# Hybrid streaming-encoder layer: y's halves split sooner, B's additions a step later, bias tiles made apart from their load, eight fillers moved to A's first step, the last tile in pieces

## The chip, the cores and the metric

The kernel runs on one core of a Trainium2 chip. The metric is the device time of one execution in microseconds (us). The engines are PE (TensorE, matmuls and transposes), DVE (VectorE), ACT (ScalarE), POOL (GpSimd) and SP (SyncE, which issues all DMAs of this kernel). Each engine works through its own queue in order.

## The reference

One post-norm layer with 1024 positions, width 1024, float32. Two token mixers run on the same input, A over bands of 9 chunks of 64 with a bias by distance, B with stick-breaking weights, 8 heads of 64 each; then gates, projections, two layer norms and a SwiGLU of width 2816.

```
h = x @ w_in[l]
qa, ka, va, qb, kb, vb, ga, gb = jnp.split(h, split_pts, axis=-1)
y_a = chunk_band_attention(heads_a(qa), heads_a(ka), heads_a(va), rel_bias[l]) @ w_proj_a[l]
y_b = stick_breaking_attention(heads_b(qb), heads_b(kb), heads_b(vb)) @ w_proj_b[l]
mix = (sigmoid(ga + b_gate[l, :D]) * y_a + sigmoid(gb + b_gate[l, D:]) * y_b) @ w_out[l]
x = layer_norm(alpha * x + mix, ln1_g[l], ln1_b[l])
g, u = jnp.split(x @ w_ffn_in[l], 2, axis=-1)
x = layer_norm(alpha * x + (silu(g) * u) @ w_ffn_out[l], ln2_g[l], ln2_b[l])
```

In `chunk_band_attention` the scores get `bias = rel_bias[:, idx]` with the clipped distance as index, then a softmax. In `stick_breaking_attention` the weight of position s at t is sigmoid(z_ts) times the product of (1 - sigmoid(z_tj)) over s < j < t; each is then multiplied with v.

## The kernel before

**Precision.** Every float32 operand is split into a high part (ACT casts it to fp32r) and a low part (DVE or POOL subtracts the high part from the raw one), and a product is three matmuls: high by high, high by low, low by high. `split`, line 108, does this with ACT and DVE; `split_y`, line 798, with ACT and POOL.

**Stages.** In order of time: the input projections (to about 343 us of the span), the attention of 16 heads (to about 660), the projection of B and the output projection with the first layer norm, the SwiGLU's upward part, and its downward part with the second layer norm, eight tiles of 128 rows each, at the end.

**The attention.** The loop at line 856 goes over 16 heads (8 of A, then 8 of B) with 12 steps each: 8 steps of group 0 (queries 0 to 511) and 4 of group 1 (512 to 1023). A step stands for one block of 128 keys. Its `turn` transposes the weights of up to 4 query blocks on PE into a `tr` bank and splits the result into a `pt` tile (4 of them); its `mult` multiplies this tile with v into the single `pv` bank. A `mult` waits in `pend` until LAG = 2 later steps have been written down. At the second step of a group of A, one `mult` is popped ahead of the turn. The last `mult` of a group has ACT copy the `pv` bank (line 704), one half of the copy goes through a DMA to other partitions (line 705), and `add` has POOL add it to the rest (line 708). `add` is put off in the list `later`, whose items count down at each step, three steps before. For pairs 5 and 6 `add` puts `split_y` into the same list, 6 and 8 steps on.

The weights themselves are made ahead by `wunits`, one unit for one block of 128 queries: `soft_block` for A (scores on PE, bias and minimum on DVE, exponential on ACT, division on POOL) and `stick_block` for B (scores on PE, two sigmoids on ACT, a scan on DVE, and a product on POOL, line 649). `LEAD` says how many units are written down by each step; the fourth unit of a B head is written down at step 8 of the head before, four steps ahead of its first transpose. A's fifth to eighth are similarly early; the first block of a head is written down at step 2 of the head before.

**The bias tile of a head of A** (`rel_bias_tile`, line 577) is loaded by one DMA into a tile `braw`; ACT writes it reversed and negated into `bias`; POOL sets two corners. This is part of `load_qk`, called at step 8 for the head after the next. Both tiles come from the four `kp` slots.

**Fillers.** PE gets other matmuls in between: 480 of them, one at a time from the generator `fill_all` (line 721). The first 288 make the gates 10 to 15 (`gate`, line 473; 48 each, with the next gate's weights split half-way through each), the other 192 the projection of A's result y (line 761, `yAps`, 24 for each of 8 columns, halves LO and HI of the positions). `FILL` gives their number for each head, spread evenly over its 12 steps. The last gate lets go of the split x tiles, and `freed` puts the split halves of y0 to y3 into their slots: the lower halves while its k = 2 to 5 are done, and the upper halves by `pieces`, from which two are taken in the gate and two in the first column's projection (line 764).

**Order.** The program is written in this order, but a planner (the scheduler of the framework) sets each engine's order from it: at each point it takes the earliest written instruction that its own cost model holds ready, so that fillers and loads can move far ahead of their place. `tc.keep_in_program_order` puts an instruction behind the one written before it on its engine; `split_y` and the gates' weights use it. The order on an engine is then fixed.

**The end.** `down_plain` (line 1151) makes a tile of 128 rows in two halves of 512 columns, 12 matmuls each; DVE adds each half to the residual. `layer_norm` (line 930) has DVE take statistics of the two halves, POOL raise the variance to the power -1/2, and, for the last tile (`quick`), DVE finish each half, which a DMA then stores.

Of the kernel before, what the change touches and what calls it, by code (L numbers as in the profile page):

```python
# [18 lines left out]
P = 128  # L19
# [18 lines left out]

FILL = (18, 18, 18, 18, 18, 18, 18, 36, 42, 42, 40, 40, 40, 38, 38, 38)

# [7 lines left out]
def hybrid_trunk_kernel(ctx: ExitStack, tc, x, xt, w_in, b_gate, rel_bias, w_proj,  # L48
# [424 lines left out]
    def gate(i, w, half_way, freed=None):  # L473
# [13 lines left out]
        if freed is None:  # L487
            for hf in range(2):
                if hf:
                    acc.append(bank("mm", f"gps{i}_1"))  # L490
                    half_way()
                for k in range(KT):
                    yield from part(hf, k)
                take(hf)
        else:
            half_way()
            for k in range(6):
                for hf in range(2):
                    yield from part(hf, k)
                freed(k)  # L500
            for hf in range(2):
                for k in (6, 7):
                    yield from part(hf, k)
                take(hf)
                freed(6 + hf)
        dma(g_dr[i], gt)
# [33 lines left out]
    def load_qk(hd):  # L540
# [11 lines left out]
        if hd["br"] == 0:  # L552
            hd["bias"] = rel_bias_tile(hd["n"])

# [21 lines left out]

    def rel_bias_tile(head):
        braw = slot("kp", f"braw{head}")
        src = rel_dr[head:head + 1, 0:640]
        dma(braw[:, 0:640],  # L580
            bass.AP(tensor=src.tensor, offset=src.offset, ap=[[1, P], [1, 640]]))
        bias = slot("kp", f"bias{head}")
        nc.scalar.activation(bias[:, 0:640], braw[:, 0:640][:, ::-1], AF.Copy, scale=-1.0)  # L583
        nc.gpsimd.memset(bias[0:DH, 576:640], BIG)  # L584
        nc.gpsimd.memset(bias[DH:P, 0:DH], BIG)
        return bias

# [65 lines left out]
    def value_steps(hd, g, wt):  # L653
# [9 lines left out]
        for i, kb in enumerate(kbs):  # L663
# [14 lines left out]
            def mult(i=i, kb=kb, lo_q=lo_q, n=n, pts=pts):  # L678
# [8 lines left out]
                if last:  # L687
# [10 lines left out]
                    else:  # L698
# [8 lines left out]
                        def add():  # L707
                            nc.gpsimd.tensor_tensor(yt[r, gs], yt[r, gs], yv[r, gs], ALU.add)
                            if h == 1 and g == 1:
# [3 lines left out]
                                else:  # L713
                                    dma(y_dr[hd["i"]], yt)
                        later.append([3, add])

# [4 lines left out]
    def fill_all():  # L721
# [23 lines left out]
        for cc in range(4):  # L745
            if cc < 3:
                end = begin_proj(0, cc + 1)
            for j in range(2):
# [5 lines left out]
                for hf, cs in enumerate((LO, HI)):  # L754
# [3 lines left out]
                    for k in range(4):  # L758
                        ks = slice(j * HW + k * P, j * HW + (k + 1) * P)
                        for n, (lw, rx) in enumerate(((w[0], yh), (w[0], yl), (w[1], yh))):  # L760
                            mm(acc, lw[:, ks], rx[k][:, cs], start=(k == n == 0),  # L761
                               stop=(k == 3 and n == 2))
                            yield 1.0
                        if k % 2 and pieces:
                            pieces.pop(0)()
# [86 lines left out]
    goal = 0.0  # L852
    load_qk(heads[0])
    load_qk(heads[1])
    load_v(heads[0])
    for si, (hd, g, st, box) in enumerate(vsteps):
        hidx, pos = si // nhead, si % nhead
        if hidx < 14 and pos == 8:
            load_qk(heads[hidx + 2])
        if pos == 4:  # L860
            if hidx < 15:
# [5 lines left out]
        while wi < min(hidx * 8 + LEAD[hd["br"]][pos], len(wunits)):  # L867
            wunits[wi]()
            wi += 1
        if st == 0:  # L870
            steps_of[(hidx, g)] = value_steps(hd, g, box)
# [10 lines left out]
        pend.append(mult)  # L882
        if len(pend) > LAG:
            pend.pop(0)()
# [44 lines left out]

    def layer_norm(t, g, b, name, quick, done=lambda cs: None):  # L930
        st = sml.tile([P, 12], F32, name=f"bn_{name}", tag="bn")
        mv = sml.tile([P, 3], F32, name=f"mv_{name}", tag="mv")
        for hf in range(2):
            nc.vector.bn_stats(st[:, 6 * hf:6 * hf + 6], t[:, hf * HW:(hf + 1) * HW])
        nc.vector.bn_aggr(mv[:, 0:2], st)
        nc.vector.tensor_scalar(mv[:, 2:3], mv[:, 1:2], EPS, None, ALU.add)  # L936
# [213 lines left out]

    def down_plain(hs, tt, evac):
        ts_ = slice(tt * P, (tt + 1) * P)
        for hf, cs in enumerate((LO, HI)):
            acc = bank("mm" if hf == 0 else "tr", f"fps{hs[0][0].name}_{tt}_{hf}")
            mm3(acc, [(hh[:, ts_], hl[:, ts_], oh[:, cs], ol[:, cs]) for hh, hl, oh, ol in hs])
            evac(acc_t[tt][:, cs], acc)
# [101 lines left out]
    for tt in range(8):  # L1258
        down_plain(last, tt, add_to)
        layer_norm(acc_t[tt], *norm2, f"2_{tt}", tt == 7,  # L1260
                   lambda cs: dma(out[tt * P:(tt + 1) * P, cs], acc_t[tt][:, cs]))

# [33 lines left out]
```

## Time and profile before

| | |
|---|---|
| median of three runs | 1446.99 us (1446.37 to 1449.32) |
| profiled execution, its own time | 1448.6 us |
| its span | 1446.8 us |
| mean granted clock of TensorE over it | 0.998 |
| busy shares: PE, DVE, ACT, POOL | 99%, 71%, 47%, 19% |

Times in the profile's rows are us from the span's start. A row of a timeline gives the start, the duration, engine and line, the operation with its output and input, its shape, and in brackets the idle time of the engine before it with what ended it. A row of the waits says which engine and line waited for which, how long in all, how often, and the longest. A row of windows gives busy time of each engine in a stretch of the span, and the granted clock. Matmuls overlap in the rows: their ends are modelled, and the distance of starts is what a matmul costs. A group's row (line, engine, operation, shapes) gives the busy time in all and the mean in ns, then the idle time before it.

### The profile page before, as it was taken

The numbers are of one execution on the slowest core, as the hardware profiler recorded it, in microseconds if no ns is written. First come the engines' busy times: TensorE is split into PE (matmuls) and PEld (weight loads), VectorE is DVE, ScalarE is ACT, GpSimd is POOL, SyncE is SP. The second block draws the span as 40 slices with busy tenths as digits, with TensorE's granted clock in tenths as the row PEclk, the third lists the DMA queues.
The fourth block names the chain that finished last, engine by engine and source line by source line (L and its number), as shares of the span: only waits on it lengthen the run. The fifth ranks groups of instructions, "written<-read, shape, count | busy, mean of one in ns | idle before, by whom it ended". The sixth has DMA issues, their size and how long they took to land.

```text
span 1446.8 us, 19239 instructions
## 1 busy us (share of the span) xinstructions
PE 1428.1 (99%) x6748; PEld 1182.8 (82%) x6748; DVE 1029.5 (71%) x1649; ACT 679.5 (47%) x1193; POOL 269.2 (19%) x329
## 2 busy tenths in 40 slices
PE   9999999999999999999999999999999999999997
PEld 7888888888788887888888888888888888888886
DVE  8875566545777777886759966776777755988767
ACT  6444444545878787773413633444444433221201
POOL 0000000001555777860004000000000000100016
PEclk9999999999999999999999999999999999999999
DMA  7555657758767477858602133444444457787502
GB/s 248 156 179 175 174 178 230 264 188 243 213 200 201 137 244 227 255 174 288 206 30 88 56 115 113 142 158 160 160 149 154 148 200 252 291 310 239 206 15 102
DMA packets 87777, 262.95 MB, mean 182 GB/s; under 512 B 10992, under 2 KB 10992, under 8 KB 87680
## 3 DMA queue, kind: packets, MB, share of 16 engines
q1 hardware_dynamic: 87680, 261.72, 54.7%
q8 instruction: 53, 0.87, 0.2%
q14 instruction: 44, 0.36, 0.1%
HBM read 169.89 MB, written 88.11 MB: 178 GB/s over the span
## 4 chain that ended last, share of the span: by engine, by line
PE 93%; DVE 3%; ACT 1%; issue 1%; DMA 1%; POOL 0%; SPq 0%; POOLq 0%; DVEq 0%; ACTq 0%
PE sxf L179 16%; PE sxp L179 11%; PE szf L179 8%; PE dx L1228 6%; PE szp L179 5%; PE syf L179 4%; PE gps L480 4%; PE syp L179 3%; PE dz L1228 3%; PE yAps L761 3%; PE tp_b L672 2%; PE ops L116 2%; PE ops L119 2%; PE ops L117 2%; PE tp_a L672 2%; PE fpswh_h L119 2%
## 5 line engine op out<-in xcount | busy, mean ns | idle before, releaser
L1184 POOL TENSOR_TENSOR wdyt<-wdyt 128x512 f32<-128x512 f32 x8 | 11.2, 1394 | 512.3 <-ACT h L1057 422.6
L649 POOL TENSOR_TENSOR w_b<-w_b,kp_b 128x511 f32<-128x511 f32 (+3 forms) x96 | 96.1, 1013 | 36.9 <-DVE kp_b L644 18.0
L644 DVE TENSOR_TENSOR_SCAN kp_b<-kp_b,ident_ps 128x512 f32<-128x512 f32 (+2 forms) x64 | 56.5, 884 | 27.0 <-ACT kp_b L641 26.6
L641 ACT ACTIVATE kp_b<-sc_b 128x512 f32<-128x512 f32 (+3 forms) x96 | 48.0, 500 | 34.7 <-PE sc_b L567 32.3
L937 POOL TENSOR_TENSOR mv<-mv,neghalf 128x1 f32<-128x1 f32 x16 | 23.9, 1495 | 207.8 <-DVE mv L936 207.8
L194 DVE TENSOR_TENSOR c<-sxp,c 128x512 f32<-128x512 f32 x16 | 11.1, 691 | 72.0 <-PE sxp L179 43.1
L584 POOL MEMSET bias<- 64x64 f32 x8 | 1.2, 144 | 326.9 <-ACT bias L583 326.9
L179 PE MATMUL szf<-x1S63h,wcf 128*128 128x512 f32 x168 | 55.1, 389 | 0.0
L110 DVE TENSOR_TENSOR pt_b<-tp_b,pt_b 128x512 fp32r<-128x512 f32 (+1 forms) x96 | 50.0, 544 | 6.3 <-ACT pt_b L109 5.6
L1159 DVE TENSOR_TENSOR x<-dx,x 128x512 f32<-128x512 f32 x64 | 43.4, 686 | 14.9 <-PE dx L1228 14.9
L614 POOL TENSOR_SCALAR w_a<-w_a,st_a 128x640 f32<-128x640 f32 (+2 forms) x64 | 42.4, 667 | 58.2 <-PE sc_a L567 25.1
L109 ACT CAST pt_b<-tp_b 128x512 fp32r<-128x512 f32 (+1 forms) x96 | 47.2, 500 | 10.3 <-PE tp_b L672 9.9
L110 DVE TENSOR_TENSOR pt_a<-tp_a,pt_a 128x512 fp32r<-128x512 f32 (+1 forms) x96 | 45.0, 486 | 9.6 <-ACT pt_a L109 8.8
L110 DVE TENSOR_TENSOR sl<-h,sl 128x512 fp32r<-128x512 f32 x56 | 38.4, 685 | 18.8 <-ACT sl L109 18.8
L109 ACT CAST sl<-h 128x512 fp32r<-128x512 f32 x56 | 34.7, 619 | 33.2 <-PE syf L179 17.1
L117 PE MATMUL ops<-wl_o,mh 128*128 128x512 f32 x128 | 50.1, 391 | 0.0
L119 PE MATMUL ops<-wh_o,ml 128*128 128x512 f32 x128 | 49.9, 390 | 0.0
L116 PE MATMUL ops<-wh_o,mh 128*128 128x512 f32 x128 | 49.7, 391 | 0.0
L609 ACT ACTIVATE w_a<-w_a,st_a 128x640 f32<-128x640 f32 (+2 forms) x64 | 44.7, 700 | 9.3 <-DVE st_a L603 6.9
L1057 ACT ACTIVATE h<-sxf 128x512 f32<-128x512 f32 x21 | 12.5, 597 | 77.1 <-PE sxf L179 77.1
L672 PE MATMUL tp_b<-ident,w_b 128*128 128x128 f32 x288 | 47.7, 275 | 0.8 <-DVE pt_b L110 0.6
L642 ACT ACTIVATE w_b<-sc_b 128x511 f32<-128x511 f32 (+3 forms) x96 | 48.1, 501 | 0.0
(1888 smaller groups left out, 4829.7 us busy)
## 6 DMA issues: line engine op xcount, KB each, us to landing
s_dr<-sl SPq DMA_DIRECT2D x112, 256.0 KB, 2.3
sd<-s_dr SPq DMA_DIRECT2D x56, 512.0 KB, 4.9
wLf<-in_w_ffn_in_dram SPq DMA_DIRECT2D x22, 512.0 KB, 4.4
wRf<-in_w_ffn_in_dram SPq DMA_DIRECT2D x22, 512.0 KB, 3.6
wRp<-in_w_in_dram SPq DMA_DIRECT2D x17, 512.0 KB, 5.5
wLp<-in_w_in_dram SPq DMA_DIRECT2D x17, 512.0 KB, 5.9
v_dr<-v SPq DMA_DIRECT2D x16, 512.0 KB, 4.1
v<-v_dr SPq DMA_DIRECT2D x16, 512.0 KB, 4.4
```

What stands on the lines that cost most here:

```text
L109: nc.scalar.copy(dst_h, src)
L110: nc.vector.tensor_tensor(dst_l, src, dst_h.bitcast(F32), ALU.subtract)
L116: mm(acc, lh, rh, start=(i == 0), stop=False)
L117: mm(acc, lh, rl, start=False, stop=False)
L119: mm(acc, ll, rh, start=False, stop=(i == n))
L179: mm(acc, lw[:, ks], rx, start=(first and kt == i == 0), stop=(kt == 3 and i == 2), skip_group_check=not first)
L480: mm(acc[hf], lw[:, ks], rx[k][:, (LO, HI)[hf]], start=(k == j == 0), stop=(k == KT - 1 and j == 2))
L642: nc.scalar.activation(be[:, m0:e], sc[:, m0 - c0:n], AF.Sigmoid)
L644: nc.vector.tensor_tensor_scan(kp[:, 0:e], kp[:, 0:e], ident_ps()[:, 0:e], 0.0, ALU.mult, ALU.add)
L649: nc.gpsimd.tensor_tensor(be[:, m0:e], be[:, m0:e], kp[:, m0 - 1:e - 1], ALU.mult)
L672: tr(tp[:, (qb - lo_q) * P:(qb - lo_q + 1) * P], wt[qb - q0][:, (kb - qb) * P:(kb - qb + 1) * P], ident)
L1228: mm(acc, a, b, start=(first and i == n == 0), stop=(i == n - 1 == 1), skip_group_check=not first)
```

## The change

- `gate`, last gate: the four upper halves of y0 to y3 are now taken from `pieces` after the first half's k = 7, after its copy, after the second half's k = 6, and after the second half's k = 7 and its copy. Nothing is left for the first column's projection.
- `add` is put off by 3 steps in A and by 4 in B.
- `rel_bias_tile` issues the DMA and returns a function that does the rest, with ACT's part kept in program order. For the first two heads it is called at once, for heads 2 to 7 through `later`, so that it runs at step 11 and not at step 8.
- 8 fillers are drawn before the first turn of the first head; heads 7 to 11 have 2, 2, 2, 1 and 1 fewer.
- In group 1 of a head of A, the step with st = 2 pops no `mult`; the next step pops two.
- The last tile of 128 rows is made in pieces of 512, 256 and 256 columns, and its statistics are taken in four quarters.

```diff
-FILL = (18, 18, 18, 18, 18, 18, 18, 36, 42, 42, 40, 40, 40, 38, 38, 38)
+FILL = (18, 18, 18, 18, 18, 18, 18, 34, 40, 40, 39, 39, 40, 38, 38, 38)
+AHEAD = 8
...
             for hf in range(2):
                 for k in (6, 7):
                     yield from part(hf, k)
+                    if k + hf == 7:
+                        freed(7)
                 take(hf)
-                freed(6 + hf)
+                freed(6 + 2 * hf)
...
         if hd["br"] == 0:
-            hd["bias"] = rel_bias_tile(hd["n"])
+            hd["end_bias"] = rel_bias_tile(hd)
...
-    def rel_bias_tile(head):
+    def rel_bias_tile(hd):
+        head = hd["n"]
         braw = slot("kp", f"braw{head}")
         src = rel_dr[head:head + 1, 0:640]
         dma(braw[:, 0:640],
             bass.AP(tensor=src.tensor, offset=src.offset, ap=[[1, P], [1, 640]]))
-        bias = slot("kp", f"bias{head}")
-        nc.scalar.activation(bias[:, 0:640], braw[:, 0:640][:, ::-1], AF.Copy, scale=-1.0)
-        nc.gpsimd.memset(bias[0:DH, 576:640], BIG)
-        nc.gpsimd.memset(bias[DH:P, 0:DH], BIG)
-        return bias
+
+        def end():
+            bias = hd["bias"] = slot("kp", f"bias{head}")
+            tc.keep_in_program_order(
+                nc.scalar.activation(bias[:, 0:640], braw[:, 0:640][:, ::-1], AF.Copy, scale=-1.0))
+            nc.gpsimd.memset(bias[0:DH, 576:640], BIG)
+            nc.gpsimd.memset(bias[DH:P, 0:DH], BIG)
+        return end
...
-                        later.append([3, add])
+                        later.append([3 + hd["br"], add])
...
-                        if k % 2 and pieces:
+                        if k == 1 and pieces:
                             pieces.pop(0)()
...
-    load_qk(heads[0])
-    load_qk(heads[1])
+    for hd in heads[:2]:
+        load_qk(hd)
+        hd["end_bias"]()
...
             load_qk(heads[hidx + 2])
+            if hidx < 6:
+                later.append([4, heads[hidx + 2]["end_bias"]])
...
+        if si == 0:
+            goal += AHEAD
+            fill_until(goal)
...
         pend.append(mult)
-        if len(pend) > LAG:
+        wait = hd["br"] == 0 and g == 1 and st == LAG
+        while len(pend) > LAG + wait:
             pend.pop(0)()
...
-    def layer_norm(t, g, b, name, quick, done=lambda cs: None):
-        st = sml.tile([P, 12], F32, name=f"bn_{name}", tag="bn")
+    def layer_norm(t, g, b, name, quick, done=lambda cs: None, n_st=2):
+        st = sml.tile([P, 24], F32, name=f"bn_{name}", tag="bn")
         mv = sml.tile([P, 3], F32, name=f"mv_{name}", tag="mv")
-        for hf in range(2):
-            nc.vector.bn_stats(st[:, 6 * hf:6 * hf + 6], t[:, hf * HW:(hf + 1) * HW])
-        nc.vector.bn_aggr(mv[:, 0:2], st)
+        w = D // n_st
+        for j in range(n_st):
+            nc.vector.bn_stats(st[:, 6 * j:6 * j + 6], t[:, j * w:(j + 1) * w])
+        nc.vector.bn_aggr(mv[:, 0:2], st[:, 0:6 * n_st])
...
-    def down_plain(hs, tt, evac):
+    def down_plain(hs, tt, evac, cuts=((0, HW), (HW, D))):
         ts_ = slice(tt * P, (tt + 1) * P)
-        for hf, cs in enumerate((LO, HI)):
-            acc = bank("mm" if hf == 0 else "tr", f"fps{hs[0][0].name}_{tt}_{hf}")
+        for n, (c0, c1) in enumerate(cuts):
+            cs = slice(c0, c1)
+            acc = bank(("mm", "tr", "sc")[n], f"fps{hs[0][0].name}_{tt}_{n}")[:, 0:c1 - c0]
...
-        down_plain(last, tt, add_to)
-        layer_norm(acc_t[tt], *norm2, f"2_{tt}", tt == 7,
-                   lambda cs: dma(out[tt * P:(tt + 1) * P, cs], acc_t[tt][:, cs]))
+        end = tt == 7
+        down_plain(last, tt, add_to, ((0, HW), (HW, 768), (768, D)) if end else ((0, HW), (HW, D)))
+        layer_norm(acc_t[tt], *norm2, f"2_{tt}", end,
+                   lambda cs: dma(out[tt * P:(tt + 1) * P, cs], acc_t[tt][:, cs]),
+                   4 if end else 2)
```

## The prediction

> **What bounds the kernel now.** I read the page's head, then TensorE's own waits, then windows of busy time over stretches of the span, and the timelines of the engines around each wait.
>
> ```profile
> span 1446.8 us, 19239 instructions
> PE 1428.1 (99%) x6748; PEld 1182.8 (82%) x6748; DVE 1029.5 (71%) x1649; ACT 679.5 (47%) x1193; POOL 269.2 (19%) x329
> ```
>
> TensorE is busy for 99% of the span, so only what makes it wait, or slows it, can be won. This execution took 1448.6 us, 1.8 us around its span, and 1.6 us over the median of the three runs (1446.99). The sum below is made against 1448.6. A difference of 0.2% (2.9 us) is about what a measurement of this kernel can tell from none.
>
> ```profile
> PE yAps L761 <- POOL yl L805: 3.4, 1, 3.4
> PE pv_a L685 <- ACT yt L704: 1.6, 4, 0.8
> PE tp_a L672 <- POOL w_a L614: 0.4, 1, 0.4
> PE pv_a L685 <- ACT pt_a L109: 0.4, 1, 0.4
> PE pv_a L685 <- ACT yv_a L704: 0.3, 2, 0.2
> ```
>
> These are the waits of TensorE that the change can touch (us in all, times, longest): one of 3.4 us for a split half of y, one at A's first step, and small ones in A's heads.
>
> ```profile
> core 0: us, PE busy (x) PEld busy (x) DVE busy (x) ACT busy (x) POOL busy (x), PEclk, DMA share, GB/s
> 370.00:466.00 96.00, 93.85 (x572) 79.96 (x572) 71.01 (x259) 75.19 (x191) 55.15 (x76) 1.00 0.72 204
> 490.00:562.00 72.00, 71.77 (x403) 61.43 (x404) 57.07 (x80) 58.40 (x138) 57.37 (x77) 1.00 0.67 210
> 562.00:586.00 24.00, 20.58 (x108) 17.35 (x107) 16.03 (x25) 14.37 (x36) 16.72 (x24) 0.93 0.79 252
> ```
>
> The windows say where there is something to win. In A's heads (370:466) TensorE idles 2.15 of 96 us; in B's heads (490:562) 0.23 of 72; in the one window after that, 3.42 of 24, and only there the granted clock is under 1: 7% of 24 us, 1.7 us of work lost.
>
> **The late half of y.** First the stall itself, on TensorE, then POOL's and ACT's rows ahead of it.
>
> ```profile
> 562.12 0.40 PE L761 MATMUL yAps<-yh,wyl 128*128 128x512 f32 x1
> 562.35 0.40 PE L761 MATMUL yAps<-yh,wyh 128*128 128x512 f32 x1
> 562.58 0.27 PE L672 MATMUL tp_b<-ident,w_b 128*128 128x128 f32 x1
> 566.27 0.65 PE L761 MATMUL yAps<-yl,wyh 128*128 128x512 f32 x1 [3.42 <-POOL yl L805]
> ...
> 567.36 0.63 PE L761 MATMUL yAps<-yh,wyl 128*128 128x512 f32 x1
> ```
>
> ```profile
> 559.14 0.67 ACT L803 CAST yh<-yraw 128x512 fp32r<-128x512 f32 x1
> ```
>
> ```profile
> 557.87 1.30 POOL L805 TENSOR_TENSOR yl<-yraw,yh 128x512 fp32r<-128x512 f32 x1
> 561.43 1.29 POOL L708 TENSOR_TENSOR yt<-yt,yv_b 64x512 f32<-64x512 f32 x1 [2.26 <-DMA yv_b<-yt]
> ...
> 562.72 2.21 POOL L649 TENSOR_TENSOR w_b<-w_b,kp_b 128x383 f32<-128x383 f32 x2
> ...
> 564.96 1.25 POOL L805 TENSOR_TENSOR yl<-yraw,yh 128x512 fp32r<-128x512 f32 x1
> ```
>
> ACT had cast the last upper half by 559.8. Its difference on POOL stands in the queue behind the addition L708, which itself waits 2.26 us for the DMA of B's value rows, and then behind two multiplications of 2.21 us together; it ends at 566.2 and TensorE goes on. The matmuls after it last 0.63 us where they lasted 0.40.
>
> Two edits meet here. In `gate` the four upper halves are now split after the first half's k = 7, after its copy, after the second half's k = 6 and after k = 7, so that all are traced before the first A projection. Before, the last two came 6 and 12 fillers into it. At 39/12 = 3.25 fillers a step the last one is traced 12 fillers or 3.7 steps sooner, ahead of the addition instead of behind it. And `3 + br` makes the addition a step later:
>
> ```profile
> L704 ACT COPY yt<-pv_b x6: 587/590/732, 500.4 to 601.0; 128x512 f32<-128x512 f32 x6
> ```
>
> These copies (first and last of six) end group 0 of head 8 and group 1 of head 12, four heads and four steps apart: 100.6 us / 52 = 1.9 us a step, which covers most of the 2.26. So the split is freed twice over. Worth: 3.4 of wait and 1.7 of clock, 5.1; the other end is 0, if the split is late again. I take 5.1: raw rows of y are loaded whole, and their lower half had been split already, so the last half is late only by its place in the order.
>
> [...]
>
> What it costs: the same four casts (0.67) and differences (1.3) come in a clump. Casts of pt on ACT and multiplications w_b on POOL behind them are up to two casts (1.3 us) and three differences (3.9) later. A B block is issued at least four steps (7.6 us) before its transposes, so I take 0.4, between 0 and 1.3. POOL is busy 57.37 of 72 us there, so it can catch up.
>
> **A's products held a step.** In A, group 1, the first product is now popped with the second, one step later. It is this product that waits for ACT's copy out of the only pv bank:
>
> ```profile
> 394.79 0.50 PE L685 MATMUL pv_a<-pt_a,v 128*128 128x512 f32 x1 [0.16 <-ACT yt L704]
> ...
> 458.61 0.50 PE L685 MATMUL pv_a<-pt_a,v 128*128 128x512 f32 x1 [0.77 <-ACT yt L704]
> ```
>
> ```profile
> 394.18 0.56 ACT L704 COPY yt<-pv_a 128x512 f32<-128x512 f32 x1
> ```
>
> These two rows are four heads apart: 63.8 / 4 = 16.0 us a head, 1.33 us a step. The copy ends at 394.74 and the product starts 0.05 later; a step more hides 0.16 to 0.77 wholly. Waits of this kind add up to 1.6 + 0.3 = 1.9. No instruction is added. Two products then stand side by side, and the fourth transpose of the group needs the fourth of the four pt tiles (rival c). Bounds: -1.9, and +1.3 if a wait of 0.16 comes to each of eight heads at the next place. I take -1.9, since the copy is queued on ACT before the held product is traced.
>
> **The bias tile.** ACT's reversed copy and POOL's two sets move from the load (step 8) to step 11, pinned behind what ACT had been given. In before the planner had floated one copy ahead of its data:
>
> ```profile
> 385.03 0.74 ACT L583 ACTIVATE bias<-braw 128x640 f32<-128x640 f32 x1 [1.92 <-DMA braw<-rel_dr]
> ```
>
> ```profile
> 385.24 0.48 PE L480 MATMUL gps<-xh,wh_g 128*128 128x512 f32 x1
> 386.08 0.39 PE L685 MATMUL pv_a<-pt_a,v 128*128 128x256 f32 x1 [0.36 <-ACT pt_a L109]
> ```
>
> ACT stood 1.92 us for the DMA, the pt casts behind it were late, and TensorE lost between the 0.36 of its row and 0.84 - 0.23 = 0.6 from start to start (0.23 is the distance of 562.12 and 562.35). Step 11 is 4.0 us after the load's step, and the copy can no longer float ahead, so ACT finds the row landed: -0.6. The load itself is issued where it was, so SP's queue is as before. The two bias tiles made before the first head are pinned too, but only behind the gate weights' cast, long before the scores. The tile is needed by the scores of step 2 of the next head, three steps or 4.0 us on; the bound above is +2.2, a wait of 0.36 like this one in each of six heads (worked out under the rivals).
>
> **Eight fillers ahead of A's first transposes**, taken from heads 7 to 11.
>
> ```profile
> 351.30 0.40 PE L480 MATMUL gps<-xl,wh_g 128*128 128x512 f32 x1
> 352.10 0.55 PE L672 MATMUL tp_a<-ident,w_a 128*128 128x128 f32 x3 [0.41 <-POOL w_a L614]
> ```
>
> Here 0.80 pass for a filler of 0.23: 0.6 lost while POOL divides the first weights. Eight fillers are 1.9 us of cover: -0.6. Bounds -1.2 (the same again within the first head) and +0.6 (the next gates' weights, their DMAs on SP, cast and difference, all come 8 fillers sooner; a new wait like this one). Where they are taken from, at most 1.9 us of TensorE work is missing; B idles 0.23 of 72 us there, so I take 0, with +1.9 as the bound if that cover is gone.
>
> **The last tile in pieces.**
>
> ```profile
> 1438.96 0.69 DVE L1159 TENSOR_TENSOR x<-fpswh_h,x 128x512 f32<-128x512 f32 x1 [0.99 <-PE fpswh_h L119]
> 1439.68 0.69 DVE L934 BATCH_NORM_STATS2 bn<-x 128x6 f32<-128x512 f32 x1
> ```
>
> ```profile
> 1438.30 2.35 POOL L946 TENSOR_TENSOR x<-x,ln2b 128x1024 f32<-128x1024 f32 x1 [1.26 <-ACT x L945]
> 1441.02 1.46 POOL L937 TENSOR_TENSOR mv<-mv,neghalf 128x1 f32<-128x1 f32 x1 [0.37 <-DVE mv L936]
> ```
>
> ```profile
> L110 DVE TENSOR_TENSOR v<-vtp,v 128x256 fp32r<-128x256 f32 x32 | 12.9, 421 | 2.6 <-ACT v L109 2.4
> ```
>
> After the last matmul DVE works 0.69 + 0.69 on 512 columns; on 256 a like operation takes 0.42: 0.54 less. Twelve matmuls more, at half the length, cost some 0.2. Two more statistics lie under the matmuls. But POOL is with the tile before until 1440.65, so its power can move from 1441.02 by 0.37 at most. I take -0.3, between -0.4 and +0.2.
>
> **Additions one step later in the other B heads**: 0; nothing in TensorE's list waits for them. What is behind them goes a step later too: on SP the store of y4, whose reload comes over a head later, and the splits of y5 and y6, which are read after the last head.
>
> **Sum**: -5.1 + 0.4 - 1.9 - 0.6 - 0.6 - 0.3 = -8.1, and 1448.6 - 8.1 = 1440.5.
>
> **Rivals.** (a) Only the stall goes. All of A is ordered anew by the planner, and waits of 0.2 to 0.8 come back at other places: the three A terms fall out, 1448.6 - 5.1 + 0.4 - 0.3 = 1443.6. For it: ACT is busy 75.19 of 96 us in A, so a new place is easily found; against: the waits recur at one place in every head, and that place gets a whole step.
>
> (b) The change doesn't do what it says: the clump of splits makes POOL late for w_b, and TensorE waits at a transpose instead. POOL's 3.9 us stand against a slack of 7.6: POOL would have to be 3.7 us behind already, and the split at 564.96, 5.2 us after its cast ended, shows that it can be. Then 1440.5 + 5.1 = 1445.6, up to 1446.5 with the clump at 1.3.
>
> (c) Slower, through the held product. With it all four pt tiles are in use at the end of group 1, and the next head's first cast on ACT waits for a tile; ACT's queue, and DVE's behind it, stands. The price is up to a step, 1.33 us, in eight heads: 10.6, with the 1.9 not won: 1440.5 + 1.9 + 10.6 = 1453.0. It decides from 0.94 us a head on (8 x 0.94 = 7.5 over 1442.4 is 1449.9). For it: four tiles, and TensorE follows ACT closely (0.05 us at 394.79). Against: the two products are emitted before the next head's transposes, and take 4 x 0.23 us at most.
>
> A like price lies in the bias: its copy 0.74 and an addition in front of its sets on POOL.
>
> ```profile
> L708 POOL TENSOR_TENSOR yt<-yt,yv_a 64x512 f32<-64x512 f32 x16 | 20.6, 1284 | 11.4 <-DMA yv_a<-yt 5.9 <-DMA yt<-yv_a 5.0
> ```
>
> Addition 1.28 and its wait 11.4 / 16 = 0.7 make 2.7 of the 4.0 us; it bites only where that DMA is over 1.3 us later still.
>
> **How the numbers follow.** The forecast 0.56, on its own 1437 to 1442.5; (a) 0.18; (b) 0.11; (c) 0.15. Faster by over 0.2% is below 1444.1: the forecast and nine tenths of (a), 0.72. Within 0.2%: (b) and the rest of (a), 0.13. Slower 0.15. The range is 1437.0 to 1448.0. Below, rows of matmuls overlap (0.40 long, 0.23 apart), so that each of nine waits may cost 0.17 more than its row shows, 1.5, with 0.6 more at the first step, the clump's 0.4, and some tenths of the stall itself: 1440.5 - 3 and a little. Above, it holds (a) and (b) and leaves out (c).
>
> **What would show it.** Right: no wait of yAps for yl, no stretch below clock 1 in the middle of the span, POOL's last upper-half difference ahead of its L708; no pv_a wait for ACT L704; ACT with no idle before L583; the last tile's statistics 0.3 sooner. Wrong: a wait of a transpose for w_b near 560, ACT idle before L109 at the heads' starts, DVE L603 waiting for the bias sets, or TensorE idle in heads 7 to 11.

## The result and the profile after

The changed kernel took 1444.46 us (median of twelve executions, 1443.25 to 1446.71), the kernel before 1447.96 beside it (1446.11 to 1450.54): ratio 0.9977, interval 0.997 to 0.9985, so 3.5 us less, where 7 to 8 had been forecast. A second set of runs, told below, gave 1443.84 beside 1448.16, ratio 0.9971 (0.996 to 0.9982).

The profiled execution of the changed kernel was its slowest, 1446.71 us. Its page's head, then TensorE's waits (who waited for whom, us in all, times, longest):

```profile
span 1444.9 us, 19255 instructions
PE 1427.9 (99%) x6760; PEld 1182.8 (82%) x6760; DVE 1030.9 (71%) x1652; ACT 679.2 (47%) x1193; POOL 269.4 (19%) x329
...
PE sc_a L569 <- DVE st_a L610: 1.9, 2, 1.7
...
PE sc_a L570 <- DMA kl<-k_dr: 1.0, 1, 1.0
PE tp_a L679 <- POOL w_a L621: 1.0, 2, 0.7
...
PE pv_a L693 <- DVE pt_a L111: 0.7, 1, 0.7
```

The wait of yAps for yl and those of pv_a for ACT's copies are gone. New are four waits in A's first heads. The same stretches as before show where:

```profile
370.00:466.00 96.00, 93.17 (x570) 80.76 (x569) 72.00 (x265) 74.59 (x194) 55.33 (x75) 0.98 0.73 204
490.00:562.00 72.00, 71.90 (x405) 61.26 (x404) 57.36 (x79) 59.05 (x139) 60.31 (x81) 1.00 0.68 209
562.00:586.00 24.00, 24.00 (x136) 20.26 (x135) 21.30 (x31) 17.44 (x41) 19.26 (x27) 1.00 0.93 293
```

562:586 is full (it idled 3.42 us and ran at 0.93), B's heads idle no more than before, and A's, which should have gained, idle 2.83 us instead of 2.15 and have a clock of 0.98: the stall and the stretch at half clock (0.50 from 567 to 569 us in the kernel before) are gone from y's half, and a new pair stands at A's third head, whose first scores are made while the second head's products run. POOL, DVE and TensorE there:

```profile
369.58 1.27 POOL L715 TENSOR_TENSOR yt<-yt,yv_a 64x512 f32<-64x512 f32 x1
370.82 2.37 POOL L449 TENSOR_TENSOR wl_g<-wr_g,wh_g 128x1024 fp32r<-128x1024 f32 x1
373.14 0.14 POOL L591 MEMSET bias<- 64x64 f32 x1
373.33 0.15 POOL L592 MEMSET bias<- 64x64 f32 x1
```

```profile
373.51 0.49 DVE L610 CUSTOM_DVE_ANT_0 w_a<-sc_a,bias 128x320 f32<-128x320 f32 x1 [2.96 <-POOL bias L592]
```

```profile
374.07 0.42 PE L569 MATMUL sc_a<-kh,qs 128*128 128x320 f32 x1 [1.71 <-DVE st_a L610]
...
375.38 0.50 PE L693 MATMUL pv_a<-pt_a,v 128*128 128x512 f32 x1 [0.75 <-DVE pt_a L111]
...
376.65 0.63 PE L481 MATMUL gps<-xh,wh_g 128*128 128x512 f32 x1
```

POOL's two sets of the third head's bias tile stand behind the addition of A's value rows and behind the low part of the next gate's weights. DVE, which adds this tile to the scores, waits 2.96 us; TensorE gets no score bank and no split weights, 1.71 and 0.75; after it the clock is 0.50 from 377 to 379 us, and matmuls of 512 columns last 0.63, where they lasted 0.40. The prediction had named this among the signs that it was wrong: DVE waiting for the bias sets. The other two new waits lie in the first head. There ACT stands for the second head's row of distances, with the first head's work behind it:

```profile
345.23 0.74 ACT L590 ACTIVATE bias<-braw 128x640 f32<-128x640 f32 x1 [2.46 <-DMA braw<-rel_dr]
```

### The profile page after: what moved, and what is told of

Its sections match the earlier page's. It is cut to its first block, busy times and chain, and to the rows that moved or that the text cites. A ratio compares the mean times of both kernels' runs of the same rounds, so it can differ in the third digit from the quotient of the medians.

```text
span 1444.9 us, 19255 instructions
## 1 busy us (share of the span) xinstructions
PE 1427.9 (99%) x6760; PEld 1182.8 (82%) x6760; DVE 1030.9 (71%) x1652; ACT 679.2 (47%) x1193; POOL 269.4 (19%) x329
## 4 chain that ended last, share of the span: by engine, by line
PE 92%; DMA 3%; DVE 2%; ACT 1%; POOL 1%; issue 1%; SPq 0%; POOLq 0%; DVEq 0%; ACTq 0%
PE sxf L180 16%; PE sxp L180 11%; PE szf L180 8%; PE dx L1244 6%; PE szp L180 5%; PE gps L481 4%; PE syf L180 4%; PE dz L1244 3%; PE syp L180 3%; PE yAps L768 3%; PE tp_b L679 2%; PE tp_a L679 2%; PE ops L117 2%; PE ops L120 2%; PE ops L118 2%; PE dy L1244 2%
```

## The experiments

Each kernel ran beside the kernel before (median 1448.2 to 1448.6 in each set); a difference under some 0.1% can't be told.

### Parts taken out of the changed kernel

`c1_bias_back` has `rel_bias_tile` whole at step 8 again, unpinned. `c1_first_two_free` takes the pin off the copies of heads 0 and 1 only:

```diff
-            tc.keep_in_program_order(
-                nc.scalar.activation(bias[:, 0:640], braw[:, 0:640][:, ::-1], AF.Copy, scale=-1.0))
+            rev = nc.scalar.activation(bias[:, 0:640], braw[:, 0:640][:, ::-1], AF.Copy, scale=-1.0)
+            if head > 1:
+                tc.keep_in_program_order(rev)
```

`c1_no_ahead` takes out the eight fillers (`AHEAD = 0`, the old `FILL`); `c1_neither` takes out the fillers and the bias edit.

> The changed kernel with the bias tiles made at their load again and unpinned, all else as changed. Theory B (the bias edit costs at A's start: the pinned early tiles hold ACT for 2.46 us of a DMA, and the late corner sets on POOL hold DVE for 2.96 us, TensorE for 1.71 and 0.75, and the clock for 1.7): 1438 to 1439.5, 5 to 6 us under the changed kernel, no stretch below clock 1 inside. Theory F (the eight fillers are to blame, since they bring the gate weights' difference of 2.37 us on POOL forward): also better, but only by the second stall, 1440 to 1441, with ACT's first exponential still late. Theory P (the planner only moves the loss): within 1 us of the changed kernel.

> The changed kernel with the pin taken off the first two heads' reversed copies alone; later ones as changed. Theory B: the first exponential comes 2.5 us sooner, TensorE's waits of 1.03 (kl) and 0.66 (w_a) in A's first step go, 1442.5; the second stall stays, with its half-clock stretch. If the order at A's start is not on the path: 1444.5.

> The changed kernel without the eight fillers ahead and with the old numbers of fillers for each head. Theory F: the gate weights' difference falls behind the bias sets again, so the stall of 1.71 + 0.75 and the half-clock 1.7 go, and the first wait for w_a costs 0.6 more: 1440.5 to 1441.5. Theory B without F: 1444 to 1445.

> The changed kernel with neither the bias edit nor the eight fillers. Theory B: 1439 to 1440.5, slightly over the one with the bias edit alone undone (0.6 for the wait at A's first transposes, 0.6 for ACT's wait for a bias row). Theory P: 1442 to 1446.

Measured: 1439.99 (ratio 0.9944, 0.993 to 0.9957) and 1439.94 (0.9944, 0.9931 to 0.9956) with the bias edit or only its first two pins undone; 1442.66 (0.9962, 0.995 to 0.9975) without the fillers; 1443.39 (0.9971, 0.996 to 0.9982) without both. The first lies between the ranges of two theories, the second under both expectations, the third between its two, and the fourth in the range of the theory that the planner only moves the loss. Two things follow. The bias edit costs 4.5 us; all of it goes with the pin on the first two copies, and it is there only with the fillers (without them the edit is 0.7 on the good side, which is inside the intervals). And the fillers are worth 3.4 us once the bias edit is out (1443.39 to 1439.99), not the 0.6 of the sum.

### Parts alone, on the kernel before

`c2_split_alone` has the edit of `gate` (the one at `pieces` then finds nothing left to take), `c2_add_alone` has `3 + hd["br"]`, `c2_hold_alone` the held product, `c2_tail_alone` the last tile in pieces, each as in the change's diff.

> The kernel before, with only the four upper halves of y split sooner. By the prediction's first term: no wait of yAps for yl, no half-clock stretch near 566, 4 to 5 us under the kernel before, 1442.5 to 1443.5. If the splits in a clump only move the wait to the transposes (rival b): within 1 us of the kernel before.

> The kernel before, with only B's additions a step later. If the addition's 2.26 us for the DMA in front of the split is what makes the half late: the split now stands ahead of the addition, and nearly the same is won as by the splits, 1442.5 to 1444. If POOL was late for other reasons: half of the 3.4 us stays, 1445 to 1446.

> The kernel before, with only the first product of A's group 1 held a step. By the prediction: the waits of pv_a for ACT's copy go, 1.9 less, 1445.5 to 1446.5, the stall at yAps as before. By rival (c): ACT waits for a pt tile at the heads' starts, up to 8 us more.

> The kernel before, with only the last tile in pieces of 512, 256 and 256 and four statistics. By the prediction 0.3 us less from the last tile's first matmul to the end; in the time not to be told from the kernel before, in the rows from the first matmul of the last tile to the end of the span 0.2 to 0.4 less.

Measured: the split 1443.43 (0.9967, 0.9955 to 0.9979), the addition 1447.44 (0.9994, 0.9986 to 1.0003), the held product 1447.0 (0.999, 0.9981 to 0.9998), the tail 1448.43 (1.0, 0.9992 to 1.0009). The split came out as expected; the addition and the held product won less than any theory had for them. POOL in the split's and in the addition's profile, with TensorE's row and window of the latter:

```profile
555.44 1.29 POOL L807 TENSOR_TENSOR yl<-yraw,yh 128x512 fp32r<-128x512 f32 x1
561.53 1.28 POOL L710 TENSOR_TENSOR yt<-yt,yv_b 64x512 f32<-64x512 f32 x1 [1.89 <-DMA yv_b<-yt]
```

```profile
559.97 1.28 POOL L708 TENSOR_TENSOR yt<-yt,yv_b 64x512 f32<-64x512 f32 x1 [1.20 <-DMA yv_b<-yt]
...
561.25 2.24 POOL L649 TENSOR_TENSOR w_b<-w_b,kp_b 128x383 f32<-128x383 f32 x2
...
563.52 1.26 POOL L805 TENSOR_TENSOR yl<-yraw,yh 128x512 fp32r<-128x512 f32 x1
```

```profile
564.83 0.50 PE L761 MATMUL yAps<-yl,wyh 128*128 128x512 f32 x1 [2.39 <-POOL yl L805]
...
562.00:586.00 24.00, 21.61 (x123) 18.16 (x122) 18.22 (x27) 15.75 (x39) 18.25 (x26) 1.00 0.85 264
```

With the split sooner the last difference ends five us ahead of the addition, which still waits, for nobody. With the addition a step later it waits 1.20 and not 2.26, but the split is behind it as before, and TensorE waits 2.39. So the split's place alone takes the stall away; the addition's does not. The tail shows in the rows only: POOL's power starts 7.37 us after the last tile's first matmul and not 7.70, the 0.3 that was forecast. The held product, in the profile's waits:

```profile
PE tp_a L672 <- DVE pt_a L110: 1.2, 2, 0.8
PE pv_a L685 <- ACT yt L704: 0.5, 1, 0.5
```

1.6 of pv_a for ACT become 0.5, and 0.4 of tp_a for DVE become 1.2: 1.1 us of the wait are won and 0.8 of that are given back at a transpose (0.78 at 458.00 us, where the product had waited 0.77 at 458.61). By the ratio the edit is worth 1.4 us, with an interval of 0.3 to 2.7.

### The stall at the third head

`d_after_again` is the changed kernel unchanged. `d_loads_first` issues both early loads before the first tile is ended, and keeps all pins; `d_end_step10` ends the later tiles a step sooner, and keeps the late load:

```diff
     for hd in heads[:2]:
         load_qk(hd)
+    for hd in heads[:2]:
         hd["end_bias"]()
```

```diff
-                later.append([4, heads[hidx + 2]["end_bias"]])
+                later.append([3, heads[hidx + 2]["end_bias"]])
```

> The changed kernel unchanged, for a second profile of it. In the first one TensorE lost some 2.4 us in the first head (0.66 for a division, 1.03 for a load of k, and what stands around them), 1.71 + 0.75 at the first scores of the third head, and then 1.7 to a half clock of 3.4 us. That profile was the slowest of twelve executions (1446.71; median 1444.46). Theory: the stalls are there in every execution and the half clock only in some, so 1444.5 again, the same two waits at 344 to 351 and at 374 to 376 us, and a clock of 1 behind them. Rival: the profiled execution was odd as a whole, and the stall at 374 us is absent from this one; then the 4.5 us between this kernel and the one with the first two copies let free have another place.

> As the changed kernel, but the loads for the first two heads are both issued before the first bias tile is ended: the second row of distances goes out beside the first, at some 313 to 323 us of the span, and not at 334 behind the six loads of q and k. Both copies on ACT stay pinned behind the cast of the gate weights, and POOL's order is the one of the changed kernel, the sets of the third head's tile behind the addition and the gate weights' difference. Theory 1, the pin costs only through the load that it holds back: ACT stands no 2.46 us at 343, the first head is on time and the queue on POOL at 370 has its slack again, so 1440.0 as with the two copies free. Theory 2, the stall at the third head has its own cause, POOL's order: the first head's 2.4 us come back and 1.7 + 0.75 stay, so 1442. Theory 3, the place of the copies on ACT itself costs: 1444.5 still.

> As the changed kernel, with the tiles of heads 2 to 7 ended at step 10 and not at 11. Up to the third head's tile nothing differs, the second row of distances is still loaded at 334 us; but POOL's two sets of the third head's tile then stand ahead of the addition of A's value rows (1.27) and the gate weights' difference (2.37), and not behind them. Theory 1, all follows from the late load: the first head loses 2.4 us, DVE still waits at 373, and the time stays at 1444. Theory 2, two mechanisms that add: DVE's wait of 2.96 at 373 goes, TensorE keeps its 1.71 + 0.75 us there, and the time is 1442.0. Rival: the copy on ACT, a step sooner, stands for its DMA again, and TensorE has new waits of 0.4 in some heads: 1444 or more.

Measured: 1443.84 (1442.33 to 1446.96), 1440.76 (0.9948, 0.9935 to 0.996) and 1440.15 (0.9941, 0.9928 to 0.9953). In the second profile of the changed kernel ACT's early copy has no wait and the first head is on time, yet the third head stalls as before, with a half clock (0.83 on the mean of 366 to 376 us). POOL and DVE of this profile:

```profile
342.29 0.72 ACT L590 ACTIVATE bias<-braw 128x640 f32<-128x640 f32 x1
```

```profile
360.89 0.81 POOL L621 TENSOR_SCALAR w_a<-w_a,st_a 128x640 f32<-128x640 f32 x1 [6.70 <-DVE st_a L620]
...
366.91 1.28 POOL L715 TENSOR_TENSOR yt<-yt,yv_a 64x512 f32<-64x512 f32 x1
368.16 2.36 POOL L449 TENSOR_TENSOR wl_g<-wr_g,wh_g 128x1024 fp32r<-128x1024 f32 x1
...
370.67 0.15 POOL L592 MEMSET bias<- 64x64 f32 x1
```

```profile
370.85 0.49 DVE L610 CUSTOM_DVE_ANT_0 w_a<-sc_a,bias 128x320 f32<-128x320 f32 x1 [3.00 <-POOL bias L592]
```

The same with the loads first:

```profile
359.56 0.81 POOL L621 TENSOR_SCALAR w_a<-w_a,st_a 128x640 f32<-128x640 f32 x1 [5.28 <-PE tp_a L679]
...
366.52 2.40 POOL L449 TENSOR_TENSOR wl_g<-wr_g,wh_g 128x1024 fp32r<-128x1024 f32 x1
...
369.06 0.15 POOL L592 MEMSET bias<- 64x64 f32 x1
```

```profile
369.24 0.49 DVE L610 CUSTOM_DVE_ANT_0 w_a<-sc_a,bias 128x320 f32<-128x320 f32 x1 [0.81 <-POOL bias L592]
```

And with the tiles ended at step 10:

```profile
361.65 0.81 POOL L621 TENSOR_SCALAR w_a<-w_a,st_a 128x640 f32<-128x640 f32 x1 [7.22 <-DVE st_a L620]
...
367.48 0.15 POOL L592 MEMSET bias<- 64x64 f32 x1
367.71 1.28 POOL L715 TENSOR_TENSOR yt<-yt,yv_a 64x512 f32<-64x512 f32 x1
368.95 2.40 POOL L449 TENSOR_TENSOR wl_g<-wr_g,wh_g 128x1024 fp32r<-128x1024 f32 x1
```

The causes do not add; the stall needs all of them at once. With the loads first POOL's order is the same, but its divisions for the second head begin 1.33 us sooner and the sets end 1.6 sooner; DVE comes 0.6 later and waits 0.81, which TensorE doesn't feel. With step 10 the divisions are the latest of the three, but the sets are ahead of the 3.6 us of addition and difference, and DVE never waits for them. The fillers ahead are a third condition: without them (`c1_no_ahead`) the divisions are as late (361.57), but the difference begins at 373.57, long after the sets at 363.87, and the stall is absent. That the gate weights' difference comes sooner with the fillers stands in the prediction, as their bound of +0.6. Each cure alone brings 3.1 and 3.7 us back beside the 1443.84 of the same set (3.7 and 4.3 beside 1444.46), so the expectation of 1442 for either was wrong, and so was that of 1444 for the second; the 1440.0 of the first theory for the loads was near. What makes the second head late is the queue on SP. In the changed kernel the second row of distances is loaded behind the first head's q and k, after the first copy (328.97 to 329.70), and the third row and the second head's k follow later and in another order:

```profile
333.80 0.58 SPq L584 DMA_DIRECT2D braw<-rel_dr  x1
...
345.43 0.38 SPq L584 DMA_DIRECT2D braw<-rel_dr  x1
345.91 0.75 SPq L554 DMA_DIRECT2D kl<-k_dr  x1
347.90 1.09 SPq L554 DMA_DIRECT2D kh<-k_dr  x2
349.04 0.59 SPq L554 DMA_DIRECT2D kl<-k_dr  x1
```

With the loads first:

```profile
320.92 0.32 SPq L584 DMA_DIRECT2D braw<-rel_dr  x1
...
345.50 1.50 SPq L554 DMA_DIRECT2D kl<-k_dr  x2
```

The last piece of kl goes out 2 to 3 us later in the changed kernel, and the second head's first products with kl stand at 356.66, behind a wait of the weight load for this DMA, and not at 356.03. Why SP's order changes so isn't shown. The end of the copy alone doesn't hold the load: in the kernel before it goes out (321.56) while the copy still runs (320.97 to 321.71). Shown is that it goes late when it is written behind a pinned copy, and early when either the pin or that place is changed (321.38 in `c1_first_two_free`). The half clock, expected in some executions only, is in both profiles (0.83 over 10 us in each, from 370 us in the first and from 366 in the second). What only one of the two has is ACT's 2.46 us: the load issued at 334.16 landed 11 us later in the first profile, the one issued at 333.80 within 8.5 in the second.

### The fillers

`e_ahead_alone` is the kernel before with `AHEAD = 8` and the new `FILL`, nothing else. `e_lead_given_back`, on the step-10 version, takes the eight from heads 0 to 6 and not from 7 to 11. `e_no_hold` is the step-10 version without the held product. `f_fill_in_a` is the kernel before with the eight spread over A and none ahead:

```diff
-FILL = (18, 18, 18, 18, 18, 18, 18, 36, 42, 42, 40, 40, 40, 38, 38, 38)
+FILL = (20, 19, 19, 19, 19, 19, 19, 34, 40, 40, 39, 39, 40, 38, 38, 38)
```

> The kernel before with the eight fillers ahead of A's first transposes and the smaller numbers for heads 7 to 11, nothing else. In the changed kernel without the bias edit the fillers were worth 3.4 us (1443.39 to 1439.99), and 0.6 had been predicted for one wait at the first step, which is still there in every profile with them. Theory 1, the fillers give the whole of A a lead of 1.9 us over ACT, DVE and POOL: small waits of 0.2 to 0.9 all through the eight heads go also without the other edits, so the time is 3 us under the kernel before: 1445.2, with the stall of yAps at 566 us unchanged. Theory 2, they only work with the held product, whose two matmuls then have a place to stand: 1447.6, 0.6 under before. Rival: the next gates' weights, brought forward, meet the bias sets on POOL as in the changed kernel: 1448 or more.

> As the version with the tiles ended at step 10 (1440.15), but the eight fillers ahead are taken from heads 0 to 6 (16, 17, 17, 17, 17, 17, 17), and heads 7 to 11 keep their old numbers. Theory 1, it is a lead, used up as the heads go by: what the first heads win stays, the later ones lose it again, so about half of the 3.4 us is gone: 1441.9. Theory 2, the place counts (the first step, and the order that the planner makes from it): 1440.2. Theory 3, the gain is that of the smaller numbers in heads 7 to 11, not of the fillers ahead: 1443.5.

> As the version with the tiles ended at step 10 (1440.15), without the held product: in group 1 of A the products are popped one a step, as before. Alone the held product was worth 1 to 1.5 us (1447.0 beside 1448.4, a difference of the profiles of 1 in waits). Theory 1, the terms add: 1441.2 to 1441.9, with waits of pv_a for ACT's copy back. Theory 2, the lead of the eight fillers covers the same waits, and the two edits are worth the same thing once: 1440.2. Rival: without the two products side by side it is faster, below 1439.8.

> The kernel before, with the same eight fillers taken from heads 7 to 11, but spread over heads 0 to 6 (20, 19, 19, 19, 19, 19, 19) and none put ahead of the first step. The fillers ahead alone gave 1439.55, 9.0 under the kernel before: 3.9 us less lost in A's heads and 5.3 less at the half of y, whose last split then stands ahead of the addition on POOL. Theory 1, the number counts: A's heads lack work for TensorE while B's do not, and wherever in A the eight stand, it idles less: 1439.5 to 1441. Theory 2, the place counts: only fillers ahead of the first transposes give a lead that ACT, DVE and POOL keep through all heads; spread out, each head's waits stay, and only the 5.3 at the half of y are won: 1443.3.

Measured: 1439.55 (0.9944, 0.9931 to 0.9958), 1445.07 (0.9978, 0.997 to 0.9987), 1441.05 (0.9952, 0.994 to 0.9964), 1440.3 (0.9947, 0.9933 to 0.996). The eight fillers alone do more than the whole change, 9.0 us, against all three expectations. TensorE over A in the kernel before, with the fillers ahead, and with the fillers spread over A:

```profile
340.00:466.00 126.00, 122.61 (x738) 103.62 (x737) 92.85 (x345) 99.25 (x248) 67.64 (x95) 1.00 0.72 203
```

```profile
340.00:466.00 126.00, 124.45 (x752) 106.24 (x752) 94.61 (x347) 101.50 (x254) 67.79 (x95) 1.00 0.72 208
...
548.00:572.00 24.00, 24.00 (x137) 20.58 (x136) 20.60 (x29) 19.21 (x46) 20.52 (x29) 1.00 0.94 285
```

```profile
340.00:466.00 126.00, 123.75 (x750) 105.58 (x749) 93.90 (x346) 100.30 (x251) 68.05 (x95) 1.00 0.71 206
```

TensorE does 14 and 12 matmuls more in the same 126 us. A rough estimate from the distances of matmuls' starts, less the columns' own time, has TensorE lose 3 to 4 us less over A's heads with the fillers ahead, and some 2 to 3 less with them spread. The stretch of y's half is full as well, because the planner now puts both of the last splits ahead of the addition on POOL:

```profile
553.84 2.54 POOL L806 TENSOR_TENSOR yl<-yraw,yh 128x512 fp32r<-128x512 f32 x2
556.34 1.29 POOL L709 TENSOR_TENSOR yt<-yt,yv_b 64x512 f32<-64x512 f32 x1
```

So the fillers' 9.0 are about 5 at this stall, which the split's edit wins too, and the rest, 3.4 to 3.9 by the runs, in A. There the number counts, not the place: spread over A they win nearly the same, and when A's later heads pay for the eight ahead, all of it is lost: 1445.07, above even the 1443.5 of the third theory, with new waits of 1.2 us for kh's load and up to 1.3 for DVE's pt, so part of this is the new order. A lacks work for TensorE and B does not. Why 1.9 us of work take away twice as much loss isn't shown; the planner's order differs throughout. The held product's 0.9 beside the fillers (1441.05 to 1440.15) is about what the theory of adding terms has, but no more than can be told.

More of them, and both cures together: `d_ahead16` has sixteen ahead with the first two copies free; `e_best` has both cures (the two diffs above) with eight ahead; `f_ahead12` is `e_best` with twelve.

> The first two copies let free (1439.94 so far), and sixteen fillers in place of eight ahead of A's first transposes, the eight more taken from heads 7 to 11 (32, 38, 38, 38, 38). With none the time was 1443.39 without the bias edit, with eight 1439.99: eight are worth 3.4 us. Theory 1, the fillers give a lead that the whole of A uses: TensorE still lost 0.7 to 1.2 us in each of the stretches of the first four heads, and eight more win 1 to 2 us: 1438.5. Theory 2, the cover was needed for one wait and is there: 1440.0. Rival: the next gate's weights, cast and difference come sooner still and get in front of the heads' own work, or B lacks the fillers (0.23 of 72 us idle there): 1441 to 1443.

> Both cures of the stall at the third head in one: the first two copies on ACT free of the pin (1439.94), and the later tiles ended at step 10 (1440.15). Theory 1, each took away the whole of the same stall, so together they win no more than the better one: 1439.9. Theory 2, each left a remnant (DVE still waits 0.81 us for the sets in the version with the loads first): 1439.2. Rival: the earlier sets stand in front of a division of the second head on POOL: 1441.

> The best of the versions with all edits so far (both cures of the third head's stall, 1439.25), with twelve fillers ahead and not eight; heads 7 to 11 have 33, 39, 39, 38, 39. Sixteen gave 1441.16, with 2 us more lost at the end of A. Theory 1, more lead still wins up to a point: 1438.7. Theory 2, eight cover what can be covered, and the order at the end of A decides: 1439.3 to 1441.

Measured: 1441.16 (0.9949, 0.9936 to 0.9963), 1439.25 (0.994, 0.9928 to 0.9953; 1439.13 to 1439.28) and 1440.63 (0.9949, 0.9937 to 0.9962): the rival's range for sixteen, and the second theory's time for the other two. More than eight wins nothing: 1.2 and 1.4 us are lost in the medians, with overlapping intervals. With sixteen TensorE idles 2.07 us from 420 to 490 us, at the end of A and the start of B, and with eight (`c1_first_two_free`) 0.68. `e_best` is the fastest kernel of the study, 8.7 to 9.3 us under the kernel before and some 5 under the change; `e_ahead_alone`, a few lines, is 0.3 behind it, which can't be told. That both cures together win 0.7 over the better one fits a remnant left by each, but is under what can be told. The waits of TensorE in `e_best` of 0.3 us or more, beside two at the program's start:

```profile
PE tp_a L680 <- DVE pt_a L111: 0.4, 1, 0.4
PE tp_a L680 <- POOL w_a L622: 0.4, 1, 0.4
PE tp_b L680 <- DVE pt_b L111: 0.3, 1, 0.3
```

## Why the prediction was wrong, point by point

The range, 1437.0 to 1448.0, held the time; the forecast of 1440.5 missed by 4 us, and the gain of 0.23% (0.15 to 0.3) is hardly more than the 0.2% that the prediction counted as the same. The sign was right, the sum was not, and two of its terms failed in opposite ways; that the time still lay in the range is in part luck, since the two errors offset each other.

- **The two early tiles, costed at nothing.** "Pinned too, but only behind the gate weights' cast, long before the scores" is the step that failed. The copy is early enough for the scores. But the load of the second row, written behind this copy, goes out at 333.80 and not at 320.92, and the second head's kl 2 to 3 us later with SP's new order. "The load itself is issued where it was, so SP's queue is as before" does not hold for these two. Together with the next point this costs 3.7 to 4.5 us (1443.84 or 1444.46 beside 1440.15 and 1439.94), and neither costs it alone.
- **The bias tile, -0.6, bound +2.2.** The mechanism beside rival (c), an addition in front of the sets on POOL, was the right one, at 2.7 of 4.0 us of slack; left out were the gate weights' difference of 2.36 in the same queue and the division of 0.70 ahead of both. 0.70 + 1.28 + 2.36 + 0.35 for the sets are 4.7, more than the slack, and the stall comes once and not in six heads. With the fillers, and without the two early pins or with step 10, the edit is worth nothing that can be told (1439.94 and 1440.15 beside 1439.99). ACT's 1.92 us for braw, which it was to win, falls to 0.5 with the fillers alone.
- **Eight fillers, -0.6, between -1.2 and +0.6.** Mis-sized: 3.4 with the stall at y's half already gone, 9.0 alone. And the wait that gave the size stayed:

```profile
351.98 0.55 PE L673 MATMUL tp_a<-ident,w_a 128*128 128x128 f32 x3 [0.39 <-POOL w_a L615]
```

  This is the first step in `e_ahead_alone`, where 0.41 was to go. The row to read was the window: 2.15 us idle in A, 0.23 in B. That B has the cover was right. Their bound of +0.6, the gate weights coming sooner, is the third part of the new stall.
- **y's half, -5.1 + 0.4.** Right: 5.2 alone (1448.6 to 1443.43), and no wait for the clump. "Freed twice over" was wrong, since the later addition alone leaves 2.39 us in its profile.
- **The held product, -1.9.** Right in kind and perhaps too large: 1.4 alone (0.3 to 2.7) and 0.9 in the company of the rest. Most of the wait went, but a transpose takes 0.8 of the 1.1 us, a wait at the next place, which had been the bound and not the value. Rival (c) fell: ACT waits for a product to let go of a pt tile once, 0.69 us at 365, as in the kernel before.
- **Additions, 0, and the tail, -0.3.** Both are inside what the times can tell; in the rows the tail's 0.33 is there. POOL's power starts at once behind its addition (1438.82 after 1438.79), as written.
- **Rivals.** (a) gives the right number, 1443.6, for a wrong reason: A's terms were not 0 but about -4.3 and +4.3. (b) fell with `c2_split_alone`: no transpose waits for w_b.

With the terms as measured, -5.2 - 3.4 - 0.9 + 4.3 is -5.2; the change has -3.5 to -4.3, and the interval of each term is over 1 us wide.

The clock: the prediction has a loss of it, 1.7 us, at the one stall of 3.42 us alone. The second profile of the changed kernel has such a loss behind shorter waits:

```profile
366.00:376.00 10.00, 7.50 (x39) 6.02 (x38) 4.97 (x23) 6.71 (x18) 7.55 (x10) 0.83 0.69 204
```

The waits there are 1.75 and 0.75 with two matmuls between them, and 0.83 over 10 us is 1.7 us lost. In `c2_add_alone` a single wait of 2.39 left it at 1.00 from 562 to 586 us. So a wait of 3.42 isn't needed, and the longest single wait doesn't decide. Whether the sum of the waits does (2.50 with, 2.39 without), these profiles can't tell.

## What to carry to other kernels

When a pin or a wait is put on an early, idle-looking instruction, look at what is written behind it: here the next load went out 13 us later, and the loads behind it in its queue later and in another order. Compare idle time by stage before reading single waits: fillers belong where TensorE idles, and moving eight of them was worth 9.0 us alone, some 5 of it by a new order at y's half, where all the other edits together won 5.7 (`c1_no_ahead`). And before costing an instruction's place in a queue, sum all that can stand ahead of it there, the work of other parts too, since delays that are harmless alone can meet.

## What the runs showed of the hardware

The granted clock fell behind a single wait of 3.42 us in the kernel before (0.93 over 562 to 586 us, 0.50 from 567 to 569), and behind waits of 1.75 and 0.75 us close together in the second profile of the changed kernel (0.83 over 366 to 376 us; matmuls of 512 columns start 0.42 apart there and 0.23 elsewhere). Behind a single wait of 2.39 us in `c2_add_alone` it was 1.00 over 24 us. The 0.83 over 10 us is a loss of 1.7 us, at a clock of 0.50 a stretch of 3.4 us, which is an estimate from these numbers. The mean clock also differs between executions of one kernel: over the 75 executions of the kernel before beside these experiments, the nine with a mean clock of 0.999 took 1446.3 us on the mean and the twenty with 0.996 took 1449.4. A loss of 1.7 us is 0.0012 of the mean, so by estimate part of the spread of this kernel (1445.7 to 1452.2) lies in how many such stretches an execution has; no run shows their number outside the profiles.

The same small load, 320 KB, issued in the same place behind six loads of q and k, landed after 11 us in one execution and within 8.5 in another; its price was 2.46 us of ACT, which only the first shows.

The stall at y's half measures 2.39 to 3.42 us for the same order on POOL behind the addition, in the profiles of the kernel before and of three single edits. Versions without a stall there or at the third head spread over 0.15 (`e_best`) to 3.1 us (`e_lead_given_back`).
